# One hand-written order for the front, the first v unit and the convolution stage of a hybrid mixer layer

## The chip, the cores and the metric

The kernel runs on one core of a Trainium2 chip. The metric is the device time of one execution in microseconds; the time of the kernel before is the median of three runs. A profile of one execution gives the instructions of each engine: PE (TensorE products), PEld (its weight loads), DVE (VectorE), ACT (ScalarE), POOL (GpSimd) and SP (SyncE, which here only issues DMAs).

## The reference, cut to what matters

One layer works on 1024 latent tokens and 256 context tokens of width 1024:

```
shift, scale, gate = split(silu(c) @ w_ada + b_ada, 3)          # context: the same with c_ctx
h  = rms_norm(x)   * (1 + scale)   + shift
hc = rms_norm(ctx) * (1 + scale_c) + shift_c
qkv_a, z_a, a_raw, b_raw, q_b, k_b, v_b, z_b, gates = split(h @ w_in)
# branch A: conv of 5 taps + silu on qkv_a, l2 norm of q and k, gated delta rule in chunks, both directions,
#           with decay from a_raw and beta from b_raw
# branch B: rms norm and rotary position of q_b, k_b, two softmax maps p0 - lam * p1 against v_b
out = x + gate * ((sigmoid(g_a) * (y_a @ w_oa) + sigmoid(g_b) * (y_b @ w_ob)) @ w_out)
```

`lam` comes from four vectors lambda_q1, lambda_k1, lambda_q2, lambda_k2, and the rotary tables from `rope` and the norm weights of q and k. All is float32; a product is made of three products of high and low halves (`hi*hi`, `hi*lo`, `lo*hi`).

## The kernel before, in words

The program is straight line code, and every engine executes its instructions in order. The order comes from one of two sources. Most of the program is ordered by a planner of the framework, which plays through an own model of the times. Sections inside `tc.manual_schedule` keep the order in which the Python code issues; there the code has *streams* (generators that yield an engine, a price in us, what the step waits for, and the instruction), and `turn_flow` takes the stream whose next step can start first by those prices, with a bias of each stream between steps of the same engine. `DV2` and `POOL` in a price mean that the two exclude each other.

The stages around the change:

- **Front** (`front`, L229). SP loads `c`, `c_ctx`, the modulation weights `w_ada` in four units (0 to 3) of two halves of 1 MB, x in tiles of 128 tokens (groups of 4, 4 and 2 tiles, the last the context), the first v weights `w`, and the small rows `rw` (b_ada, norm weights, conv_w). The letters of `"01osw23xy"` are the order of the loads. `rms(g)` squares x on ACT (L303), takes the inverse root on DVE (L180 to L185, twelve instructions with L304) and scales x (L307). `modulation(u)` multiplies c by `w_ada` on PE (L320; L318 for units 2 and 3), copies the row (L321), transposes it in another bank (L328 or L330) and adds the bias (L333, L335). `turn(g, k)` transposes one eighth of the width of a token group (L344) and modulates it: high half on ACT (L346), full value on DVE (L347), low half on DVE or POOL in turn (L348).
- **First v unit** (`tok_unit`, L422, with `before`): ten tiles of 128 tokens times 288 columns (256 of v, 32 of the decay and beta inputs), 24 products a tile. The first four tiles are taken in three parts of the width. The planner orders the front and this unit. `v_out` (L638 to L643) casts the high half on ACT, subtracts the low half on DVE and stores both.
- **Convolution stage** (`conv_start`): hand order. 24 tiles of q, k and v of branch A: products on PE, four of five taps on DVE, silu, norms, stores. Side streams are the weights, `gates()` (decay and beta, in a bank of `self.pt`) and `gate_row()`. `lam_setup` (L1406 to L1417) stands just ahead of it, in the planner's part.
- **Second v unit**: planner's order again. `gdn_first` issues the first loads and ACT's decay instructions (L1050, exponential L1052) of the scan, `qk_tables` builds the rotary tables (loads L616 and L619, small products L622, eight products L627, store L630), and `v_unit(1)` makes five banks of two tiles each, copied out through one pair of buffers `ch0`, `cl0` with the same `v_out`.
- **Scan section**: hand order again, with pieces of k, v and q of branch B between (`part_flow`), and the Gram products of the delta rule (`gram`, in `gdn_prep`).

The banks of PSUM that the front, gates and norms use were one pool of three buffers under one tag, given out in turn:

```
self.pt = self.spool(cp, "ptr", 3, space=PSUM)
...
for u in range(4):
    modulation(u)
    turn(0, 2 * u)
    turn(0, 2 * u + 1)
```

Of the kernel before, what the change touches and what calls it, by code (L numbers as in the profile page):

```python
# [8 lines left out]
F32 = mybir.dt.float32  # L9
# [8 lines left out]
P = 128  # L18
# [25 lines left out]
class Block:  # L44
# [143 lines left out]
    def setup(self):  # L188
# [30 lines left out]
        self.tbd = self.dp.tile([P, 1024], F32, name="tbd")  # L219
# [7 lines left out]
    def front(self, st, early):  # L227

        nc, a, cp = self.nc, self.a, self.cp  # L229
        fs, ft = self.spool(st, "fs", 1, side="right"), self.spool(st, "ft", 2, side="right")  # L230
        fx = [self.spool(early, "fx0", 4)] + [self.spool(st, f"fx{i}", n, side="right") for i, n in ((1, 4), (2, 2))]
        fq = self.pt
        groups = (range(0, 4), range(4, 8), range(8, NT))
        xt, wa = {}, {}
# [4 lines left out]
        def load_x(t):  # L239
            nc.sync.dma_start(xt[t], a["x"][0, t * P:(t + 1) * P, :] if t < NL else  # L240
                              a["ctx"][0, (t - NL) * P:(t - NL + 1) * P, :])

        def load_ada(u):

            for i in range(2):
                if u == 0:
                    wa[u, i] = self.wab[0].tile([P, KT, W], F32, tag=("wh", "wl")[i], name="wa")
                elif u == 1:
                    wa[u, i] = self.hc.tile([P, KT, W], F32, tag=f"s2{i}", name="wa")
                else:  # L250
                    if i == 0:
                        wa[u, 2] = self.hp.tile([P, KT, 512], F32, tag=f"s1{u - 2}", name="wa")
                    wa[u, i] = wa[u, 2][:, :, i * W:(i + 1) * W]
                nc.sync.dma_start(wa[u, i], a["w_ada"][0, :, i * D + u * W:i * D + (u + 1) * W].rearrange(
                    "(k p) n -> p k n", p=P))

        rows = fs.tile([16, P], F32, name="rows")
        nc.sync.dma_start(rows[0:8, :], a["c"].rearrange("o (k p) -> (o k) p", p=P))
        nc.sync.dma_start(rows[8:16, :], a["c_ctx"].rearrange("(k p) -> k p", p=P))
        for o in "01osw23xy":  # L260
            if o == "s":
                rw2 = fs.tile([26, P], F32, name="rw2")
                nc.sync.dma_start(rw2[0:24, :], a["b_ada"].rearrange("o (k p) -> (o k) p", p=P))
                nc.sync.dma_start(rw2[24:25, :], a["gdn_norm_w"])
                nc.sync.dma_start(rw2[25:26, :], a["diff_norm_w"])
                rw3 = fs.tile([120, P], F32, name="rw3")
                nc.sync.dma_start(rw3, a["conv_w"].rearrange("o j (k p) -> (o j k) p", p=P))
            elif o in "0123":
                load_ada(int(o))
            elif o == "w":  # L270
                self.ahead = self.load_w(self.wcols(C_VB), True)
            else:
                for t in groups["oxy".index(o)]:
                    load_x(t)
        sil = fs.tile([16, P], F32, name="sil")
        nc.scalar.activation(sil, rows, AF.Silu)
        tp = fq.tile([P, 512], F32, tag="tr", name="tp")
        nc.tensor.transpose(tp[:, 0:16], sil, self.ident[:16, :16])
        cT = self.cT = cp.tile([P, 16], F32, name="cT")
        nc.vector.tensor_copy(cT, tp[:, 0:16])  # L280
        smallT = cp.tile([P, 184], F32, name="smallT")

        def smalls():
            tp = fq.tile([P, 512], F32, tag="tr", name="tp")
            nc.tensor.transpose(tp[:, 16:42], rw2, self.ident[:26, :26])
            nc.tensor.transpose(tp[:, 64:184], rw3, self.ident[:120, :120])
            nc.vector.tensor_copy(smallT[:, 16:42], tp[:, 16:42])
            nc.vector.tensor_copy(smallT[:, 64:184], tp[:, 64:184])

        self.gdn_g, self.diff_g = smallT[:, 40:41], smallT[:, 41:42]  # L290
        self.convw = lambda j, t: smallT[:, 64 + j * 24 + t:64 + j * 24 + t + 1]
        c2 = cT.rearrange("p (s k) -> p s k", s=2)
        pad = fs.tile([P, KT, 32], F32, name="pad")
        nc.gpsimd.memset(pad, 0.0)
        nc.vector.tensor_copy(pad[:, :, 0:2].rearrange("p k s -> p s k"), c2)
# [3 lines left out]
        def rms(g):  # L299
            cnt = len(groups[g])  # L300
            ss = fs.tile([P, 4], F32, tag="ss", name="ss", bufs=2)
            for j, t in enumerate(groups[g]):
                nc.scalar.activation(junk, xt[t], AF.Square, accum_out=ss[:, j:j + 1])  # L303
            nc.vector.tensor_scalar(ss[:, :cnt], ss[:, :cnt], 1.0 / D, EPS, ALU.mult, ALU.add)  # L304
            rs = self.rsqrt(fs, ss[:, :cnt], "xr")
            for j, t in enumerate(groups[g]):
                nc.vector.tensor_scalar_mul(xt[t], xt[t], rs[:, j:j + 1])  # L307

        def modulation(u):
            mp = fq.tile([P, 512], F32, tag="tr", name="mp")  # L310
            split = u >= 2
            n = P if split else 2
            mrow = fs.tile([P, 2, W], F32, tag="mrow", name="mrow")
            for i in range(2):
                for k in range(KT):
                    if split:
                        j = k % 4
                        nc.tensor.matmul(mp[32 * j:32 * j + 32, i * W:(i + 1) * W], pad[:, k], wa[u, i][:, k], start=k < 4, stop=k >= 4)  # L318
                    else:
                        nc.tensor.matmul(mp[:2, i * W:(i + 1) * W], c2[:, :, k], wa[u, i][:, k], start=k == 0, stop=k == KT - 1)  # L320
                nc.vector.tensor_copy(mrow[:n, i], mp[:n, i * W:(i + 1) * W])  # L321
            if u == 0:
                smalls()
            mt = fq.tile([P, 512], F32, tag="tr", name="mt")
            for i in range(4):
                half = mrow[:n, i // 2, i % 2 * P:i % 2 * P + P]
                if split:
                    nc.tensor.matmul(mt[:, i * 2:i * 2 + 2], half, self.fold[:, 0:2], start=True, stop=True)  # L328
                else:
                    nc.tensor.transpose(mt[:, i * 2:i * 2 + 2], half, self.ident[:2, :2])  # L330
            m = mods[:, :, 2 * u:2 * u + 2]
            bias = smallT[:, 16:32].rearrange("p (i k) -> p i k", i=2)[:, :, 2 * u:2 * u + 2]
            nc.vector.tensor_tensor(m, mt[:, 0:8].rearrange("p (i k s) -> p i k s", i=2, k=2),  # L333
                                    bias.unsqueeze(3).to_broadcast([P, 2, 2, 2]), ALU.add)
            nc.vector.tensor_scalar_add(m[:, 1], m[:, 1], 1.0)  # L335

        def turn(g, k):
            grp, nn = groups[g], len(groups[g]) * P
            th, tl, o = self.hsel(grp[0])
            s = 1 if grp[0] >= NL else 0  # L340
            sh, sc = mods[:, 0, k, s:s + 1], mods[:, 1, k, s:s + 1]
            pt = fq.tile([P, 512], F32, tag="tr", name="pt")
            for j, t in enumerate(grp):
                nc.tensor.transpose(pt[:, j * P:(j + 1) * P], xt[t][:, k * P:(k + 1) * P], self.ident)  # L344
            hf = ft.tile([P, 512], F32, tag="hf", name="hf")
            nc.scalar.activation(th[:, k, o:o + nn], pt[:, :nn], AF.Identity, bias=sh, scale=sc)  # L346
            nc.vector.tensor_scalar(hf[:, :nn], pt[:, :nn], sc, sh, ALU.mult, ALU.add)  # L347
            (nc.vector, nc.gpsimd)[k % 2].tensor_tensor(tl[:, k, o:o + nn], hf[:, :nn], th[:, k, o:o + nn].bitcast(F32),  # L348
                                                        ALU.subtract)

        rms(0)
        for u in range(4):
            modulation(u)
            turn(0, 2 * u)
            turn(0, 2 * u + 1)
        def before(t0):
            g = 1 + t0 // 4
            if t0 in (0, 4):
                self.hgroup(g)
                rms(g)  # L360
            if g < 3:
                for k in range(t0 % 4 * 2, t0 % 4 * 2 + 2):
                    turn(g, k)
        return before
# [1559 lines left out]
```

## Time and profile before

| | |
|---|---|
| median of three runs | 2060.99 us (2059.3 to 2066.39) |
| profiled execution | 2064.51 us, span 2062.7 us |
| busy share of the span | PE 96%, PEld 84%, DVE 69%, ACT 51%, POOL 33% |
| DMA | 336.45 MB, 163 GB/s over the span |
| mean granted TensorE clock | 0.982 |

A row of a timeline is start, duration, engine, line, operation, output and inputs, and in brackets how long the engine had been idle before it and what released it. A row of a grouped view is the group, its count, busy time and mean duration (ns), then the idle time before its members. The view by stretch has busy time and count for each engine, then the granted clock, the share of the DMA engines and GB/s. Products are pipelined, so the rows of PE overlap.

### The profile page before, as it was taken

Reading aid. Unit: us, or ns where it says so; the run is one execution under the profiler, and the core shown is the slowest. Engines: PE = TensorE matmul, PEld = TensorE weight load, DVE = VectorE, ACT = ScalarE, POOL = GpSimd, SP = SyncE. Lnnn points to the kernel's source line nnn. Section 1 sums busy time; section 2 is a strip of 40 time slices with the busy share of each in tenths; the row PEclk is TensorE's granted clock in tenths of the full one; section 3 lists DMA queues with packets and bytes.
Section 4 is the critical chain, followed back from the end, with each engine's and each line's share of the span. In section 5 each row is a group of like instructions: output and inputs, shape, how many; then the busy total and the mean of one; then the engine's idle time right before and its main releaser. Section 6 shows DMA issues by size and latency. Waiting matters only on the chain.

```text
span 2062.7 us, 38349 instructions
## 1 busy us (share of the span) xinstructions
PE 1970.5 (96%) x14231; PEld 1729.1 (84%) x14231; DVE 1418.1 (69%) x3611; ACT 1053.9 (51%) x2176; POOL 686.6 (33%) x601
## 2 busy tenths in 40 slices
PE   6999999979999998999899999999899999989999
PEld 3888888879999997878778888887788888877899
DVE  3798989747876895557556786237789899864532
ACT  3443435343325543566456754448678888763210
POOL 1200000014531331323233333235566767654122
PEclk9999999989999999999999999999999999999999
DMA  9226452665446546755764764857575766326442
GB/s 313 86 84 159 123 115 75 133 178 159 140 138 210 174 157 175 238 168 199 196 218 139 245 190 131 248 146 220 140 195 133 202 172 159 103 83 203 144 154 82
DMA packets 391742, 336.45 MB, mean 163 GB/s; under 512 B 144399, under 2 KB 343665, under 8 KB 391555
## 3 DMA queue, kind: packets, MB, share of 16 engines
q1 hardware_dynamic: 328675, 274.22, 46.0%
q10 hardware_dynamic: 62880, 59.78, 9.5%
q8 instruction: 112, 1.84, 0.4%
q14 instruction: 75, 0.61, 0.1%
HBM read 222.14 MB, written 111.79 MB: 162 GB/s over the span
## 4 chain that ended last, share of the span: by engine, by line
PE 70%; DMA 10%; DVE 9%; ACT 5%; issue 3%; POOL 1%; SPq 1%; ACTq 0%; DVEq 0%; POOLq 0%
PE mm L55 37%; PE chain L55 5%; PE mo L55 4%; PE s L55 4%; PE v L55 4%; DVE S L1505 3%; PE out L55 3%; PE mm L422 3%; PE ma L55 3%; DMA hx<-in_w_in_dram 2%; ACT S L1518 2%; PE t L58 2%; DMA ma<-ma 1%; PE gram L55 1%; DMA x<-xd 1%
## 5 line engine op out<-in xcount | busy, mean ns | idle before, releaser
L55 PE MATMUL mm<-hs,wh 128*128 128x512 f32 (+1 forms) x2048 | 646.0, 390 | 0.0
L55 PEld LDWEIGHTS mm<-hs,wh 128*128 128x128 f32 x2048 | 374.1, 191 | 57.6 <-issue 0.9
L55 PE MATMUL mm<-hs,wl 128*128 128x512 f32 (+1 forms) x1024 | 401.0, 392 | 0.0
L55 PE MATMUL mm<-wh,hs 128*128 128x256 f32 x1472 | 274.1, 286 | 0.0
L1505 DVE TENSOR_SCALAR_CACHE_REDUCE S<-s,rsq 128x512 f32<-128x512 f32 (+1 forms) x384 | 241.6, 654 | 32.3 <-PE s L55 28.9
L55 PEld LDWEIGHTS mm<-wh,hs 128*128 128x128 f32 x1472 | 231.4, 192 | 0.4
L55 PEld LDWEIGHTS mm<-hs,wl 128*128 128x128 f32 x1024 | 195.0, 190 | 29.2 <-issue 0.9
L1542 POOL TENSOR_TENSOR S<-S 128x1280 f32<-128x1280 f32 x64 | 188.8, 2952 | 91.4 <-ACT S L1535 88.9
L55 PE MATMUL mm<-wl,hs 128*128 128x256 f32 x736 | 210.4, 286 | 0.0
L1518 ACT ACTIVATE S<-S,mn 128x1280 f32<-128x1280 f32 x128 | 174.7, 1366 | 34.4 <-DVE mn L1517 33.9
L55 PE MATMUL s<-kk,qh 128*128 128x512 f32 (+1 forms) x384 | 144.9, 378 | 3.6 <-DVE S L1505 3.3
L523 DVE SCALAR_TENSOR_TENSOR ac<-xc,smallT,ac 128x1284 f32<-128x1284 f32 (+1 forms) x96 | 138.9, 1448 | 11.3 <-ACT ac L521 10.5
L55 PEld LDWEIGHTS mm<-wl,hs 128*128 128x128 f32 x736 | 141.2, 192 | 0.3
L55 PE MATMUL s<-kk,ql 128*128 128x512 f32 (+1 forms) x384 | 133.6, 358 | 0.0
L1579 DVE TENSOR_TENSOR al<-t,ah 128x512 fp32r<-128x512 f32 (+1 forms) x192 | 107.6, 592 | 10.6 <-ACT ah L1574 10.0
L511 ACT COPY xc<-mm 128x512 f32<-128x512 f32 (+1 forms) x64 | 34.0, 534 | 145.9 <-PE mm L55 134.8
L1574 ACT CAST ah<-t 128x512 fp32r<-128x512 f32 (+1 forms) x192 | 89.9, 515 | 30.6 <-PE t L58 29.3
L1101 DVE TENSOR_TENSOR tmp<-ab,ts 80x31 f32<-80x31 f32 (+15 forms) x248 | 98.8, 398 | 8.4 <-DMA ab<-da 2.8
L508 POOL MEMSET xc<- 128x2 f32 (+1 forms) x64 | 3.6, 100 | 290.9 <-ACT sq L562 150.7
L58 PE MATMUL t<-ct,S 128*128 128x128 f32 x640 | 95.7, 275 | 3.2 <-POOL S L1542 1.6
L1279 DVE SCALAR_TENSOR_TENSOR S<-S,egl,chain 128x128 f32<-128x128 f32 x128 | 43.1, 344 | 76.4 <-PE chain L55 73.5
L1266 ACT ACTIVATE vd<-chain,edk 128x128 f32<-128x128 f32 x144 | 52.1, 368 | 84.6 <-PE chain L55 79.2
(280 smaller groups left out, 4804.9 us busy)
## 6 DMA issues: line engine op xcount, KB each, us to landing
wr<-in_w_in_dram ACTq DMA_DIRECT2D x42, 512.0 KB
hx<-in_w_in_dram ACTq DMA_DIRECT2D x64, 256.0 KB
X<-gcd SPq DMA_DIRECT2D x16, 640.0 KB
kd<-col SPq DMA_DIRECT2D x40, 256.0 KB
xd<-X SPq DMA_DIRECT2D x16, 640.0 KB
x<-xd SPq DMA_DIRECT2D x80, 128.0 KB
kk<-kd SPq DMA_DIRECT2D x32, 320.0 KB
wa<-in_w_ada_dram SPq DMA_DIRECT2D x8, 1024.0 KB
```

Source lines behind the costliest of these rows:

```text
L55: self.nc.tensor.matmul(out, lhsT, rhs, start=start, stop=stop)
L58: self.nc.tensor.transpose(out, src, self.ident[:src.shape[0], :src.shape[0]])
L422: nc.tensor.matmul(pt[:, j * W:j * W + n], ht[:, k, ts], wt[:, k, :n], start=k == i == 0, stop=k == KT - 1 and i == 2)
L523: t = yield DV2, 1.21e-3 * wd, [t], lambda: nc.vector.scalar_tensor_tensor(ac[:, :wd], xc[:, j:j + wd], self.convw(j, x["ct"]), ac[:, :wd] ...
L1101: t = yield DV2, n * w / 960.0 + 0.08, [t, t1], lambda: V.tensor_tensor(tv, ab[:, j + 1:, j:j + 1].to_broadcast([80, n, w]), ts[:, j, :w]. ...
L1266: td = yield ACT, 0.251, [t], lambda: nc.scalar.activation(vd, pc[:, 1], AF.Copy, scale=self.edk[:, c, g:g + 1])
L1279: t = yield DVE, 0.263, [t], lambda: V.scalar_tensor_tensor(Sn, S, self.egl[:, c, g:g + 1], pc[:, 2], ALU.mult, ALU.add)
L1505: e = yield DVE, 0.675 if m == 512 else 0.408, [e, self.sfree[c].get(n - 4 + c)], lambda: self.nc.vector.tensor_scalar(x["S"][c][:, o:o + ...
L1518: x["x"].append((yield ACT, 1.36, [e], lambda: nc.scalar.activation(S, S, AF.Exp, bias=x["mn"][:, c:c + 1], scale=-1.0, accum_out=w["l0"][ ...
L1542: e = yield POOL, 2.9, [e], lambda: self.nc.gpsimd.tensor_tensor(S0, S0, S1, ALU.add)
L1574: e = yield ACT, 0.48 if nb == 4 else 0.27, [t, y["old", k]], lambda: self.nc.scalar.copy(y["ah", k][:, :, q], pv)
L1579: t = yield DVE, 0.603 if k < 2 else 0.322, [e, y["old", k]], lambda: self.nc.vector.tensor_tensor(y["al", k][:, :, q], pv, y["ah", k][:, ...
```

## The change

The front, the first v unit and the convolution stage lie in one `manual_schedule`. Every step of the front is a stream with prices; the rotary tables and lambda become streams of the convolution stage beside the gates. In detail:

- Loads: the letters are `"0s1xw23yk"`: the small rows come after unit 0's weights, and the load of the first convolution weights (`k`, once the v weights are split) is one of them. The split of those has both low halves on DVE (before: one on POOL, one on DVE).
- Modulation: products, copy, the two transposes and the bias add of a half share one bank, half after half.
- The three banks get names (`tr0` to `tr2`) and a list `pfree` with the time from which each is free; a stream that needs one waits for the list.
- `turned` (high, full and low half) is queued by even and odd k; low halves of even k are DVE's, of odd k POOL's (as before).
- Tables: both are stored to DRAM (`tbd` has two parts); the one for k is loaded again after the convolution stage. They use the buffer `graw` of the gate row, which therefore starts after them. The gate temporaries `gtmp` and `gr` share a buffer.

```
-                        self.lam_setup()
...
+                    with tc.manual_schedule(engines={E.PE, E.DVE, E.Activation, E.Pool, E.SP}):
+                        with ExitStack() as st, ExitStack() as sw:
+                            self.wv = self.spool(sw, "wv")
+                            with ExitStack() as early:
+                                self.front(st, early, self.wcols(kv[0][1]))
+                        with ExitStack() as st:
...
                             self.conv_start(kv, C_VB + W)
                 first, head = self.gdn_first(gr, zr)
-                self.qk_tables()
+                tb = self.tk.tile([P, 2, 2, NL, 32], F32, tag="tb", name="tb")
+                nc.sync.dma_start(tb.rearrange("p a b t f -> p (a b t f)"), self.tbd[1])
+                self.rope["k"] = tb, None
```

The front's streams, and those of the convolution stage (the number is the bias):

```
+        for g, b in ((loads(), 0), (modulation(), 1), (smalls(), 1), (rms(), 2), (weights(), 1.5), (turns(), 1), (self.forever(turnq[0]), 1.2),
+                     (self.forever(turnq[1]), 1.2), (self.forever(evq), 3), (main(), 9)):
+            self.stream(g, b)
+        self.turn_flow(lambda: "end" in T and not evq and 0 in self.parts_)
...
-        self.stream(self.gates(), 0.5)
+        for g, b in ((self.gates(), 0.5), (self.lam_setup(), 0.6), (self.qk_tables(), 4)):
+            self.stream(g, b)
```

One half of the modulation, and the products of the v unit:

```
+                for i in range(2):
+                    yield lambda: ("wa", u, i) in T
+                    o = i * W
+                    for k in range(KT):
...
+                    t = yield DVE, 0.42, [t], lambda: V.tensor_copy(mrow[:n, i], mp[:n, o:o + W])
+                    for q in range(2):
+                        t1 = yield PE, 0.17 if u >= 2 else 0.09, [t], lambda: self.mm(
+                            mp[:, o + 2 * q:o + 2 * q + 2], mrow[:n, i, q * P:q * P + P], self.fold[:, 0:2]) if u >= 2 else self.tr(
+                            mp[:, o + 2 * q:o + 2 * q + 2], mrow[:n, i, q * P:q * P + P])
...
+        def main():
...
+                        for k in ks:
+                            yield lambda: ("h", g, k) in T and ("w", k // 4) in T
...
+                                e = yield PE, 0.133, [T["h", g, k], T["w", k // 4], b], lambda: self.mm(
+                                    pt[:, :W + 32], ht[:, k, o:o + P], wt[:, k], k == i == 0, k == KT - 1 and i == 2)
+                        if KT - 1 in ks:
+                            evq.append(evac(t, pt, e))
```

The tables as a stream:

```
+            tc.append((yield DMA, 0.4, [], lambda: nc.sync.dma_start(cs[:, i], a["rope"][i].rearrange("(t p) f -> p t f", p=P))))
+        for n, (nm, mul) in enumerate((("q", -(64.0 ** -0.5)), ("k", 1.0))):
+            g0 = tk.tile([P, 64], F32, tag="g0" + nm, name="g0")
+            t = yield DMA, 0.2, [], lambda: nc.sync.dma_start(g0, a[f"{nm}_norm_w"].to_broadcast([P, 64]))
+            t = self.later(t, 4.0)
...
+                    te = yield DV2, 0.4, [tg, tc, to], lambda: V.tensor_tensor(
+                        tb[:, i, hf], cs[:, i], g[:, hf].unsqueeze(1).to_broadcast([P, NL, 32]), ALU.mult)
+            to = yield DMA, 1.5, [te], lambda: nc.sync.dma_start(self.tbd[n], tb.rearrange("p a b t f -> p (a b t f)"))
+            to = self.later(to, 4.0)
+        self.rope, self.tb_t = dict(g=g), to
```

More of the change, by code (lines that the diff above doesn't have):

```diff
@@ L257, in front @@
[L257 to L280, printed above, removed]
-        smallT = cp.tile([P, 184], F32, name="smallT")
[L283 to L288, printed above, removed]
+        rows, rw2, rw3 = (fs.tile([n, P], F32, name=i) for i, n in (("rows", 16), ("rw2", 26), ("rw3", 120)))
@@ L309, in modulation @@
[L309 to L314, printed above, removed]
-                for k in range(KT):
[L316 to L364, printed above, removed]
+        self.pfree, self.slot_t = [(i, None) for i in range(3)], [None, None]
+        turnq, evq, wv = ([], []), [], [self.wv.tile([P, KT, W + 32], F32R, tag=t, name=t) for t in ("wh", "wl")]
@@ new lines, in evac @@
+        def evac(t, pt, e):
+            vt, old = [self.tv.tile([P, 2, W], F32R, tag=i, name="vt") for i in ("vh", "vl")], self.slot_t[t % 2]
+            e1 = yield ACT, 0.31, [e, old], lambda: nc.scalar.copy(vt[0][:, 0], pt[:, :W])
+            e2 = yield DVE, 0.38, [e1, old], lambda: V.tensor_tensor(vt[1][:, 0], pt[:, :W], vt[0][:, 0].bitcast(F32), ALU.subtract)
+            e3 = yield DVE, 0.15, [e], lambda: V.tensor_copy(self.abt[:, t], pt[:, W:W + 32])
+            free.append([e1, e2, e3])
+            self.slot_t[t % 2] = ends = []
+            for i, x in enumerate((e1, e2)):
+                ends.append((yield DMA, 0.5, [x], lambda: nc.sync.dma_start(
+                    self.vd[i, t * P:(t + 1) * P, 0:W], vt[i][:, 0].bitcast(F32))))
@@ L390, in load_w, with unit @@
         return hi, lo
[L392 to L406 removed]
+    def unit(self, src, work, then):
+        cur, self.ahead = self.ahead, self.load_w(then)
+        work(*cur)
@@ L441, in work @@
                 emit(t0, pt)
[L442 to L444 removed]
+        return self.wcols(c0), work
     CB = 5
```

391 lines of the change are left out of this document (241 added, 150 removed).

## The prediction

> **What bounds the kernel now.** I read the page first, then busy time by stretch with the cuts where the chain of waits changes its character, then the chain itself, and last the timeline of each engine in the two places that stood out.
>
> ```profile
> span 2062.7 us, 38349 instructions
> ...
> PE 1970.5 (96%) x14231; PEld 1729.1 (84%) x14231; DVE 1418.1 (69%) x3611; ACT 1053.9 (51%) x2176; POOL 686.6 (33%) x601
> ```
>
> The PE (TensorE matmul row) is busy for 96% of the span, so a change that leaves the products alone can only remove idle PE time, and idle time there moves all that follows. By stretch (us; busy time and count of PE, PEld, DVE, ACT, POOL; granted clock; DMA share; GB/s):
>
> ```profile
> 0.00:94.74 94.74, 72.90 (x483) 55.19 (x484) 52.18 (x125) 36.88 (x60) 22.35 (x20) 0.91 0.62 205
> 94.74:409.33 314.59, 314.59 (x1583) 266.00 (x1583) 274.88 (x388) 134.55 (x162) 3.61 (x64) 1.00 0.46 116
> 409.33:445.21 35.88, 35.88 (x300) 35.67 (x298) 14.61 (x16) 15.95 (x30) 5.43 (x3) 1.00 0.74 189
> 445.21:458.94 13.73, 0.00 (x1) 0.03 (x1) 8.74 (x20) 7.80 (x18) 3.65 (x2) 0.63 0.38 134
> ```
>
> The convolution stage (94.74 to 409.33) has no idle PE at all, DVE has 314.59 - 274.88 = 39.7 us to spare in it. The front with the first v unit (0 to 94.74) leaves PE idle for 21.8 us, and what is busy there runs partly at a lower clock. Between the second v unit and the scan section PE stands still for 13.73 us. These two places are what the change can touch.
>
> **The front: why it takes 92.7 us.** The nine convolution products already inside the stretch are taken off: 94.74 - 9 x 0.2265 (the order's own price of one) = 92.7 is where the v unit would have ended alone.
>
> ```profile
> L55 PE MATMUL mm<-hs,wh 128*128 128x512 f32 x6 | 2.0, 393 | 0.0
> L55 PE MATMUL mm<-hs,wl 128*128 128x512 f32 x3 | 1.2, 394 | 0.0
> ```
>
> Timeline of the front (start, duration, idle before it and its cause):
>
> ```profile
> 7.45 5.76 PE L320 MATMUL mp<-wa,cT 128*2 128x256 f32 x16 [2.18 <-DMA wa<-in_w_ada_dram]
> 13.71 3.62 PE L320 MATMUL mp<-wa,cT 128*2 128x256 f32 x16 [0.51 <-DVE mrow L321]
> 21.98 0.21 PE L285 MATMUL tp<-ct,rw 26*128 26x26 f32 x1 [4.65 <-DMA rw<-in_diff_norm_w_dram]
> 24.99 2.61 POOL L389 TENSOR_TENSOR wl<-wr,wh 128x1152 fp32r<-128x1152 f32 x1 [23.93 <-ACT wh L388]
> 25.03 2.59 DVE L185 SCALAR_TENSOR_TENSOR xry<-xrt,xry 128x4 f32<-128x4 f32 x1
> 29.58 1.41 DVE L307 TENSOR_SCALAR x<-x,xry 128x1024 f32<-128x1024 f32 x2
> 36.12 1.53 DVE L347 TENSOR_SCALAR hf<-pt,mods 128x512 f32<-128x512 f32 x2 [1.10 <-ACT hs L346]
> 37.57 0.68 DVE L348 TENSOR_TENSOR hs<-hf,hs 128x512 fp32r<-128x512 f32 x1
> 38.86 0.40 PE L422 MATMUL mm<-wh,hs 128*128 128x288 f32 x1
> 69.58 0.65 ACT L638 CAST vt<-mm 128x256 fp32r<-128x256 f32 x2 [0.98 <-PE mm L422]
> ```
>
> PE executes in order, and the order puts the small rows' transpose (L285) behind the first modulation unit: it waits 4.65 us, until 21.98, for rows that were issued behind 6 MB of weights and x. The second modulation unit (two halves of 3.62 us) comes after that and after the wait for the scaled x (ready at 30.99), so the first v product is at 38.86. The first token group is not complete until just before 69.58, when the first v tile is copied out. From there PE is continuous; the chain has it on PE from 71.32 on, 92.7 - 71.3 = 21.4 us.
>
> ```profile
> 71.32 0.67 PE mm L422 x3
> ...
> 94.74 27.35 PE mm L55 x143
> ...
> 438.13 7.08 PE mm L55 x59
> 445.21 13.73 issue
> 458.94 2.05 PE gram L55 x8
> ```
>
> **Edit 1, the front under the hand order.** Removed: the order in which PE waits for rows, for x and for DVE in turn. The small rows are issued behind 2 MB rather than 6 MB, so unit 0 ends soon after its weights. Its products run as now until 17.3. Each half now shares one bank with its two transposes, so product, copy, transposes and add alternate; the row at 13.71 shows one such hand-over at 0.51 us, four of them and the copy I take at 1.5 us a half. Unit 1 then ends at about 18.8 + 2 x (3.62 + 1.5) = 29, or 32 if its copies queue behind the DVE instruction that stalls until 27.6: either way no later than the scaled x, which stays at 31 (its chain, squares then DVE, is not changed, and the POOL split of the v weights at 24.99 still meets it). Transposes, ACT, DVE and the low half follow: first v product near 35 instead of 38.9.
>
> ```profile
> L307 DVE TENSOR_SCALAR x<-x,xry 128x1024 f32<-128x1024 f32 x10 | 6.9, 749 | 0.1
> L184 DVE SCALAR_TENSOR_TENSOR xrt<-xrt,ss 128x4 f32<-128x4 f32 x6 | 1.0, 163 | 0.2
> L321 DVE COPY mrow<-mp 128x256 f32<-128x256 f32 x4 | 1.7, 420 | 0.8 <-PE mp L318 0.8
> L639 DVE TENSOR_TENSOR vt<-mm,vt 128x256 fp32r<-128x256 f32 x8 | 3.3, 415 | 0.3 <-DMA vd<-vt 0.2
> L389 DVE TENSOR_TENSOR wl<-wr,wh 128x1024 fp32r<-128x1024 f32 x1 | 1.2, 1217 | 0.0
> L348 POOL TENSOR_TENSOR hs<-hf,hs 128x512 fp32r<-128x512 f32 x8 | 13.9, 1733 | 34.3 <-DVE hf L347 29.6 <-DVE xry L181 4.7
> ```
>
> From here DVE decides. One pair of k (rows 36.12 and 37.57) costs it 1.53 + 0.68 = 2.2 us; the first group's four pairs 8.8, units 2 and 3 about 2.4 (four copies of 0.42 and the small adds), the v weights' low half 1.4: 12.6 us, so the group is complete at 31 + 1.5 + 12.6 = 45, say 47 with some waits, instead of 69. What is then left for DVE: scaling six tiles 6 x 0.75 = 4.5, two chains of 12 small instructions at 0.16 plus gaps 4.8, the second group's pairs 8.8, the context group's about 6 (half as wide, but not half the time: I take 1.5 a pair), ten evacuations of 0.42 and 0.18 6.0, both low halves of the first convolution weights 2.4 (one of them is POOL's today): 32.5 us. About 4 of it fits in before 47. Stalls against POOL, of which the row at 25.03 is one, I put at about 4 again. DVE is through at 47 + 32.5 = 79; the last two tiles' evacuations and part of the weight split lie behind the last product, so PE ends at about 77. PE alone would take 21.4 us from 47, so 69 to 71 is the floor. Gain: 92.7 - 77 = 15.7, between 92.7 - 71 = 22 and, if the group is only complete at 54, 92.7 - 84 = 8.
>
> [...]
>
> **Edit 2, lambda, gates and rope tables as side streams of the convolution.** Moved into it: eight table products and four small ones, and their loads.
>
> ```profile
> L627 DVE TENSOR_TENSOR tb<-ropecs,g x8: 413/418/2633, 441.8 to 449.2; 128x256 f32<-128x256 f32 x8
> ...
> 430.12 4.20 SPq L616 DMA_DIRECT2D ropecs<-in_rope_dram  x2
> 434.37 3.56 SPq L619 DMA_DIRECT2D g<-in_q_norm_w_dram  x1
> 438.04 0.37 SPq L643 DMA_DIRECT2D vd<-vt  x1
> ...
> 432.77 5.97 ACT L1050 ACTIVATE X<-X,gcc 128x128 f32<-128x128 f32 x20 [10.81 <-DMA X<-gcd]
> 442.17 1.27 ACT L1052 ACTIVATE X<-X 128x1280 f32<-128x1280 f32 x1
> ...
> 441.54 0.27 DVE L622 TENSOR_SCALAR g<-g 128x32 f32<-128x32 f32 x2 [18.40 <-DMA g<-in_q_norm_w_dram]
> 458.14 0.69 DVE L639 TENSOR_TENSOR vt<-mm,vt 128x512 fp32r<-128x512 f32 x1 [2.29 <-DMA vd<-vt]
> 460.28 0.58 ACT L638 CAST vt<-mm 128x512 fp32r<-128x512 f32 x1 [2.27 <-DMA vd<-vt]
> ```
>
> In the convolution they cost DVE 8 x 0.418 + 4 x 0.135 = 3.9 us against 39.7 spare, PE nothing; if that cover were gone, 3.9. The gate row waits for the tables (one buffer), and nobody needs it before the last phase. Gates and lambda ran there or just ahead already: nothing.
>
> Where they are taken away: DVE stood for 18.40 us at L622, in front of the second v unit's first low half; SP spent 4.20 + 3.56 us on the tables' loads ahead of the first v store. Evacuations use one pair of buffers, so each waits for the store before it: from DVE's half (458.14) to the next ACT half (460.28) 2.1, plus ACT's 0.58: about 2.8 us a turn. The Gram product at 458.94 starts when the low half at 458.14 has ended: it waits for a bank of the v unit. Without the tables the first low half can follow its cast at once, and the first store leaves at 438.0 - 7.8 = 430.3 (a load of the finished table, 0.5 MB, takes their place on SP; one issue like that at 438.04 is 0.4 us). What is late next is ACT: if the 20 decay instructions and both exponentials keep their place ahead of the second cast, that comes at 443.4, and the fourth low half ends 2 x 2.8 + 0.6 + 0.7 later, near 450.5: 5.3 us of idle stay, 8.4 go. If the casts come first, all 13.7 go. I take 9 (nearer the first, as nothing moves ACT's loads).
>
> ```profile
> 460.00:470.00 10.00, 10.00 (x78) 10.00 (x78) 5.24 (x14) 4.47 (x14) 1.26 (x1) 0.88 0.42 142
> 470.00:480.00 10.00, 10.00 (x87) 9.98 (x86) 8.18 (x24) 3.54 (x8) 4.32 (x4) 1.00 0.28 91
> ```
>
> After the idle time the clock is granted at 0.88 and 78 instead of 87 products are done: 9 x 0.115 = 1 us, which goes too where the idle time does. [...]
>
> **Sum.** 15.7 + 9 + 1 = 25.7 us. The profiled execution took 2064.51 us, 1.8 around its span, and lies 3.5 above the median of 2060.99; the stretches are the same in all, so the median becomes 2060.99 - 25.7 = 2035.
>
> **Rivals.** (a) Only the front is gained: ACT's order or the v stores keep the Gram product at 459. For it: the 10.7 us of ACT work ahead of the second cast; against it: the 18.40 us of DVE are gone in any order. 2060.99 - 16 = 2045. Chance 0.13. [...] Chance 0.13. (c) Slower: DVE's wait moves along. If in the convolution the lambda, norm and table instructions stand in DVE's order ahead of loads that SP has not issued yet, DVE stops there as it did at L622, the buffers of four tiles fill, and PE stops too. One stop of 18.4 us is covered by the 39.7 spare; it decides, against the 25.7 gained, from 39.7 + 25.7 = 65 us of stops, and four loads (lambda, rope, two norms) at 18.4 each make 74: 2035 + 74 - 40 = 2069. For it: DVE is in order and the loads' times in the order are prices, not measurements; against it: the gates' loads stand in the same queue today and PE has no idle time there. Chance 0.06. (d) The two orders come out alike: 2060. Chance 0.04. The forecast: 0.64.
>
> Range: 22 + 14.7 = 37 gives 2024 at the low end; the high end takes in (a) and (b), 2051. Within 0.3% (6 us, about what a measurement tells here) is (d); slower is (c) and part of what I cannot name, 0.07; faster 0.89.
>
> **What would show it.** Right: the first convolution product near 77, PE without idle time from there to the scan section, the L622 pair in the convolution, no stretch of over 6 us without PE near 430, the Gram product within 6 us of the end of the first 48 products. Wrong: the first group's last low half after 55; PE idle in the convolution; DVE idle over 10 us there before a table product; the Gram product still behind a v low half by more than 8 us; or a gap that reappears further on, at the waits of the first scan steps.

## The result, and the profile after

The changed kernel takes 2054.59 us (median of its runs, 2049.53 to 2060.42) against 2061.38 us of the kernel before in the same runs: ratio 0.9965, interval 0.9952 to 0.9978, some 7 us faster. The forecast was 2035 with a range of 2024 to 2051.

The page after, its first lines, and the stretches, cut at the first convolution product, the end of the convolution, the end of the first products of the second v unit and the first Gram product:

```profile
span 2049.1 us, 38360 instructions
...
PE 1968.3 (96%) x14231; PEld 1726.7 (84%) x14231; DVE 1419.5 (69%) x3616; ACT 1053.8 (51%) x2176; POOL 682.3 (33%) x600
```

```profile
0.00:92.89 92.89, 74.31 (x476) 55.43 (x476) 53.83 (x131) 35.50 (x59) 17.95 (x19) 0.93 0.60 200
92.89:411.04 318.15, 316.39 (x1592) 267.39 (x1591) 277.08 (x399) 135.52 (x162) 3.55 (x64) 1.00 0.48 121
411.04:446.91 35.87, 35.87 (x299) 35.67 (x298) 12.42 (x13) 17.67 (x35) 5.46 (x3) 1.00 0.73 207
446.91:454.90 7.99, 0.01 (x2) 0.04 (x1) 5.47 (x11) 5.94 (x14) 3.66 (x2) 0.72 0.33 110
460.00:470.00 10.00, 10.00 (x84) 10.00 (x84) 7.18 (x21) 5.80 (x15) 2.79 (x2) 0.97 0.31 105
```

The front still ends at 92.9 us (before 92.7). In the convolution PE now stands idle for 1.76 us (318.15 - 316.39); before, it had no idle time there. The idle time ahead of the Gram product went from 13.73 to 7.99 us, and 84 products instead of 78 are done in the 10 us from 460. The profile after is a short execution (2050.87 us), the one before a long one (2064.51); single executions differ by several us in the later stages (below), so I read the traces up to the Gram product and the medians for the rest.

**The front.** Timeline of DVE, ACT and PE in it:

```profile
30.25 0.75 DVE L391 TENSOR_SCALAR x<-x,xry 128x1024 f32<-128x1024 f32 x1
35.61 0.81 DVE L412 TENSOR_SCALAR hf<-pt,mods 128x512 f32<-128x512 f32 x1 [1.26 <-ACT hs L409]
40.91 0.38 PE L55 MATMUL mm<-wh,hs 128*128 128x288 f32 x1
49.26 0.68 DVE L415 TENSOR_TENSOR hs<-hf,hs 128x512 fp32r<-128x512 f32 x1
49.85 1.27 DVE L383 TENSOR_SCALAR ss<-ss 128x4 f32<-128x4 f32 x1
52.83 1.23 DVE L313 TENSOR_TENSOR wl<-wr,wh 128x1024 fp32r<-128x1024 f32 x1
54.05 1.22 DVE L313 TENSOR_TENSOR wl<-wr,wh 128x1024 fp32r<-128x1024 f32 x1
55.15 0.37 ACT L442 CAST vt<-mm 128x256 fp32r<-128x256 f32 x1 [4.09 <-PE mm L55]
55.90 2.73 DVE L391 TENSOR_SCALAR x<-x,xry 128x1024 f32<-128x1024 f32 x4
69.48 0.85 PE L55 MATMUL mm<-wh,hs 128*128 128x288 f32 x2 [2.31 <-DVE hs L415]
81.71 0.41 DVE L415 TENSOR_TENSOR hs<-hf,hs 128x256 fp32r<-128x256 f32 x1
```

```profile
57.00:69.50 12.50, 6.63 (x45) 4.79 (x44) 11.49 (x25) 7.33 (x13) 4.80 (x4) 0.94 0.21 72
69.50:74.40 4.90, 4.56 (x16) 4.02 (x17) 4.72 (x11) 0.00 (x0) 1.06 (x1) 0.50 0.00 0
74.40:92.89 18.49, 18.46 (x138) 17.91 (x136) 8.26 (x23) 5.94 (x13) 3.39 (x4) 0.99 0.22 72
```

The first group is early, nearly as forecast: first full value at 35.6, first v tile copied out at 55.15 instead of 69.58. The first v product is not early: 40.91 (38.86 before), as PE's order has transposes and products of units 2 and 3 ahead of it. From 57 us on PE runs dry. The second group's x is scaled at 55.90 to 58.6, where before it was done by 55.2: its squares lie between the first group's turns, its root chain begins with a stall beside POOL (1.27 us for four elements) and lets two weight splits of 1.2 us through. The expectations below call such stalls the lock with POOL. Four of DVE's small instructions, whose likes take 0.16 us, ended within 0.02 us of one of POOL's here: 25.16 for 2.58 (POOL's split, 25.10 for 2.62), 49.85 for 1.27 (its low half, 49.42 for 1.68), 64.10 for 1.27 (64.08 for 1.28) and 66.52 for 1.05 (66.28 for 1.28); before, the rows at 24.99 and 25.03 ended so, at 27.60 and 27.62. Its turns last until 73, and the products go tile by tile, so PE gets three products for each turn: 6.63 us of work in 12.50 us, then 4.90 us at a granted clock of 0.50. The 18.49 us of products behind that are the rest, and they end at 92.9.

How much of PE's own work was left can be counted. The first row is of the kernel before, from the moment at which the forecast took its 21.4 us of remaining PE work; the second is of the change, from 47 us, where the forecast put them:

```profile
71.32:94.74 23.42, 23.42 (x175) 23.12 (x176) 14.61 (x36) 9.20 (x19) 7.26 (x7) 1.00 0.27 89
47.00:92.89 45.89, 39.65 (x272) 36.72 (x271) 33.34 (x78) 19.14 (x35) 12.24 (x10) 0.93 0.17 58
```

Before, 175 less nine of the convolution are 166 PE instructions; now 272 are left, because the first group's products run only behind its early low halves, until 57 us.

The rows of before to which this compares (timeline of the kernel before, the second group's x, and for the next part the gate row):

```profile
52.47 2.74 DVE L307 TENSOR_SCALAR x<-x,xry 128x1024 f32<-128x1024 f32 x4
...
240.35 1.02 PE L55 MATMUL mg<-gacc,ct 128*1 128x512 f32 x2
```

**The convolution.** The table steps, and the gate row that now comes behind them:

```profile
107.55 0.18 DVE L685 TENSOR_SCALAR g<-g 128x32 f32<-128x32 f32 x1
145.36 0.42 DVE L690 TENSOR_TENSOR tb<-ropecs,g 128x256 f32<-128x256 f32 x1
280.22 1.18 DVE L882 TENSOR_TENSOR wl<-wr,wh 128x1024 fp32r<-128x1024 f32 x1
281.43 0.68 DVE L667 TENSOR_TENSOR grow<-mg,grow 1x512 f32<-1x512 f32 x1
282.16 1.02 PE L55 MATMUL mg<-gacc,ct 128*1 128x512 f32 x2 [1.76 <-DVE grow L667]
```

The tables themselves cost PE nothing that these rows show. The gate row does: its second pair of products needs the bank that DVE's add (L667) empties, that add stands behind a weight split, and PE waits 1.76 us in order. Before, it ran at 240.35 with no idle time in front.

**The gap.** The chain, then ACT and DVE:

```profile
446.91 7.99 issue
454.90 2.05 PE gram L55 x8
```

```profile
434.33 5.96 ACT L1113 ACTIVATE X<-X,gcc 128x128 f32<-128x128 f32 x20 [10.66 <-DMA X<-gcd]
444.89 0.56 ACT L700 CAST vt<-mm 128x512 fp32r<-128x512 f32 x1
445.49 0.69 DVE L701 TENSOR_TENSOR vt<-mm,vt 128x512 fp32r<-128x512 f32 x1 [19.90 <-ACT vt L700]
450.52 0.57 ACT L700 CAST vt<-mm 128x512 fp32r<-128x512 f32 x1
453.39 0.58 ACT L700 CAST vt<-mm 128x512 fp32r<-128x512 f32 x1 [1.13 <-DMA vd<-vt]
454.10 0.69 DVE L701 TENSOR_TENSOR vt<-mm,vt 128x512 fp32r<-128x512 f32 x1 [2.29 <-DMA vd<-vt]
```

DVE no longer waits for a load, but for ACT: the second cast comes at 444.89, behind the 20 decay instructions and the exponentials, and the last turns wait for stores.

### The profile page after: what moved, and what is told of

Read it like the earlier page. It is cut to its first block, busy times and chain, and to the rows that moved or that the text cites. A ratio compares the mean times of both kernels' runs of the same rounds, so it can differ in the third digit from the quotient of the medians.

```text
span 2049.1 us, 38360 instructions
## 1 busy us (share of the span) xinstructions
PE 1968.3 (96%) x14231; PEld 1726.7 (84%) x14231; DVE 1419.5 (69%) x3616; ACT 1053.8 (51%) x2176; POOL 682.3 (33%) x600
## 4 chain that ended last, share of the span: by engine, by line
PE 72%; DVE 10%; DMA 8%; ACT 5%; issue 2%; POOL 1%; SPq 1%; ACTq 0%; DVEq 0%; POOLq 0%
PE mm L55 40%; PE chain L55 5%; PE mo L55 4%; PE s L55 4%; PE v L55 4%; DVE S L1569 3%; PE out L55 3%; PE ma L55 3%; ACT S L1582 2%; PE t L58 2%; DMA ma<-ma 1%; PE mm L501 1%; PE gram L55 1%; DVE al L1643 1%; DMA x<-xd 1%
## 5 line engine op out<-in xcount | busy, mean ns | idle before, releaser
L55 PE MATMUL mm<-wh,hs 128*128 128x256 f32 (+1 forms) x1632 | 313.2, 290 | 2.6 <-DVE hs L415 2.6
L55 PEld LDWEIGHTS mm<-wh,hs 128*128 128x128 f32 x1632 | 260.8, 194 | 3.8 <-DVE hs L415 3.4
L55 PE MATMUL mm<-wl,hs 128*128 128x256 f32 (+1 forms) x816 | 236.1, 289 | 0.0
L55 PEld LDWEIGHTS mm<-wl,hs 128*128 128x128 f32 x816 | 158.3, 194 | 0.3
```

What stands on the lines that cost most here:

```text
L55: self.nc.tensor.matmul(out, lhsT, rhs, start=start, stop=stop)
```

## The experiments

All kernels are compared with the kernel before in the same runs. First convolution product, idle PE ahead of the first Gram product and its start are from the profiles, in us.

| kernel | first conv. product | idle | Gram | median (before) | ratio, interval |
|---|---|---|---|---|---|
| the change | 92.89 | 7.99 | 454.90 | 2054.59 (2061.38) | 0.9965, 0.9952 to 0.9978 |
| 1 front only | 92.70 | 12.27 | 457.23 | 2062.44 (2063.96) | 0.9991, 0.9977 to 1.0005 |
| 2 tables only | 92.28 | 7.99 | 453.53 | 2057.48 (2063.96) | 0.9965, 0.9951 to 0.9979 |
| 3 four parts | 91.40 | 8.52 | 452.13 | 2057.44 (2063.96) | 0.9955, 0.9936 to 0.9973 |
| 4 late split | 91.81 | 8.27 | 454.10 | 2060.63 (2063.96) | 0.9981, 0.9962 to 1.0001 |
| 5 no chain | 88.15 | 7.99 | 451.76 | 2056.89 (2066.13) | 0.9960, 0.9946 to 0.9975 |
| 6 x early | 96.06 | 7.99 | 458.07 | 2062.12 (2066.13) | 0.9991, 0.9975 to 1.0008 |
| 7 as 3, one execution | 88.87 | 8.01 | 449.08 | 2050.77 (2066.13) | none |
| 8 two pairs | 93.47 | 0.27 | 447.77 | 2048.45 (2066.13) | 0.9921, 0.9901 to 0.9941 |
| 9 gate first | 93.47 | 8.43 | 454.17 | 2060.30 (2065.02) | 0.9974, 0.9958 to 0.9989 |
| 10 gate, pairs | 92.82 | 0.84 | 445.92 | 2052.68 (2065.02) | 0.9937, 0.9919 to 0.9955 |
| 11 gate, pairs, parts | 90.10 | 1.26 | 443.42 | 2046.25 (2065.02) | 0.9913, 0.9894 to 0.9933 |
| 12 tables, pairs | 92.43 | 0.21 | 445.90 | 2049.38 (2065.02) | 0.9932, 0.9908 to 0.9955 |
| 13 no chain, all | 89.75 | 0.40 | 442.32 | 2043.08 (2066.93) | 0.9895, 0.9868 to 0.9922 |
| 14 chain first | 91.95 | 0.41 | 444.44 | 2047.94 (2066.93) | 0.9906, 0.9879 to 0.9934 |

In kernels 2 and 12, as in the kernel before (91.90), some v products still follow the first convolution product, so their first column is about 0.8 us early against the others: 92.7 is the figure for the kernel before with that taken off.

**1 and 2, the two edits apart.** Kernel 1 is the change with `qk_tables` at its old place (lambda stays a stream); kernel 2 is the kernel before with lambda and tables as streams.

```
1  -            self.stream(... (self.qk_tables(), 4)) in the convolution
   +                self.qk_tables()                    behind gdn_first
2  +        for g, b in ((self.gates(), 0.5), (self.lam_setup(), 0.6), (self.qk_tables(), 4)):
   +            self.stream(g, b)
```

> The change without its rope tables: front, first v unit, lambda and gates under the hand order, the rope tables built where they were. My theory (in the front DVE and PE were only rearranged; PE is starved of the second token group and pays later what it gained early): first convolution product at 92.9 us as in the whole change, DVE's 18 us stand at the norm weights back at about 441, Gram product at 459, time within 2 us of the kernel before. Rival (the front did gain, and the tables in the convolution took it back): first convolution product still at 92.9 in the trace, but the convolution ends 1.5 us or more earlier than in the whole change, and the time is 3 us or more under the kernel before.

> The kernel before with only the second edit: rope tables and lambda as side streams of the convolution stage, the front in the planner's order. Theory: the Gram product comes 4 to 6 us earlier (idle PE ahead of it 8 us instead of 13.7), and the time is 4 to 7 us under the kernel before, that is the whole of what the change brings. Rival (the two edits need each other): no more than 2 us.

The front alone is within the interval of no change; the tables alone have the whole gain. So Edit 2 works, and Edit 1 is worth nothing that can be measured here.

**3, the second group's tiles in four parts of the width**, as the first group has them (run 7 is a further execution of the same kernel):

```
-for ts, parts in (...,) + tuple(((t,), (range(KT),)) for t in range(4, NT)):
+for ts, parts in (..., (range(4, 8), ((0, 1), (2, 3), (4, 5), (6, 7))), ((8,), (range(KT),)), ((9,), (range(KT),))):
```

> The change with the second token group's four tiles taken in four parts of the width, as the first group's are in three, so that PE has products of four tiles for each eighth that DVE finishes. Theory (PE in order stands at tile 4 for the last eighth while the products of tiles 5 to 7 could run): 3 tiles x 21 products x 0.133 = 8.4 us come forward, the first convolution product is at 84 to 86 instead of 92.9, and the time falls by up to 8 us against the whole change (2046 to 2050) unless it is given back at a later wait. Rival (DVE and its lock with POOL set the end of the front): first convolution product within 2 us of 92.9.

> A second look at the kernel of the third experiment (the second group's four tiles in four parts of the width), for its trace alone: the first convolution product again within 0.5 us of 91.4, the granted clock between 60 and 72 us again at 0.5 to 0.7 if the half clock belongs to this order of work, near 1.0 if it was this one execution.

The stretches from 60 and from 70 us, first of run 3, then of run 7:

```profile
60.00:70.00 10.00, 7.68 (x35) 6.05 (x34) 8.88 (x18) 5.86 (x10) 4.30 (x4) 0.59 0.19 65
70.00:80.00 10.00, 10.00 (x70) 9.72 (x70) 6.67 (x15) 2.05 (x5) 1.82 (x2) 0.90 0.01 3
```

```profile
60.00:70.00 10.00, 6.29 (x46) 5.10 (x44) 9.21 (x18) 5.80 (x10) 4.86 (x4) 1.00 0.20 67
70.00:80.00 10.00, 9.98 (x74) 9.16 (x74) 8.58 (x19) 3.65 (x7) 2.70 (x3) 1.00 0.00 1
```

One program, two executions: in run 3 PE looks busier and did 35 products at a clock of 0.59, in run 7 46 at 1.00. The first convolution product came at 91.40 and at 88.87, not at 84 to 86: the parts are worth 1.5 to 4.0 us, and the two executions, which differ in the clock, lie 2.5 us apart. The executions end 13 us apart (spans 2062.2 and 2049.0), 3.0 us of it by the Gram product (452.13, 449.08): one profile can't weigh a few us of the later stages. Neither shows the wait at the gate row (PE is busy for all of 280 to 290 us in run 3 and of 270 to 300 in run 7) although the row still follows the tables, so the wait seems to hang on where the row falls among DVE's steps.

**4, the first convolution weights' split held back until the context's turns:** `yield lambda: ("kr", 1) in T and ("h", 2, 3) in T`.

> The change with the split of the first convolution weights held back until half of the context group is turned, so that its two low halves (2.4 us of DVE) no longer stand inside the second group's inverse root. Theory: x of the second group is scaled 2.4 us earlier (56.2 instead of 58.6) and the first convolution product comes 2 to 3 us earlier. Rival (something else, the last square on ACT or POOL's lock, holds the scaling): no change in the first convolution product.

The second group's x is scaled from 52.74 instead of 55.90, but the front ends only 1.1 us earlier, below what was expected; no gain in time.

**5, the second group's x without its own root chain.** It is scaled with the first group's inverse roots; its own squares and chain run behind, for nobody. Its result leaves out the second group's own roots, so the kernel serves to measure only.

```
+                if g == 1:
+                    for j, t in enumerate(groups[g]):
+                        T["xs", t] = yield DVE, 0.69, [T["x", t], e0], lambda: V.tensor_scalar_mul(xt[t], xt[t], y0[:, j:j + 1])
```

> The change, with one dependency taken out: the second token group's x is scaled with the first group's inverse roots as soon as it has landed, and its own squares and root chain still run, behind it, for nobody (so the second group's result is not the reference's). All engines do the same work. Theory 1, the front's end hangs on the second group's scaled x (ready at 58.6 us in the profile of the change, 55.2 before): x scaled by 48 to 51, the second group's turns run in 51 to 65 instead of 59 to 73, first convolution product at 84 to 86 instead of 92.9, time 6 to 8 us below the change (2047 by a before of 2061). Rival 2, DVE's total of work sets it: the work is the same, first convolution product at 91.5 to 93, time as the change. Rival 3, PE's order and half clock set it: as in the four-part kernel, 1 to 2 us earlier.

With the same work for every engine the front ends 4.7 us earlier, at 88.15: the late x is one limit, and not DVE's sum of work alone; 84 to 86 was too much. The time is that of the change. Part of it was lost again in the convolution, at the gate row (PE's timeline, then the 4 us behind the wait):

```profile
277.43 1.02 PE L55 MATMUL mg<-gacc,ct 128*1 128x512 f32 x2 [1.77 <-DVE grow L674]
```

```profile
278.00:282.00 4.00, 4.00 (x13) 3.05 (x12) 3.96 (x5) 1.05 (x1) 0.00 (x0) 0.58 1.20 303
```

Here the same wait is followed by a clock of 0.58. From the first convolution product to the end of the stage this execution takes 319.6 us, the profile of the change 318.0, and those of kernels 9 and 10, without the wait, 316.2: 3.4 us are lost here, 1.8 in the change.

**6, the second group's x loaded ahead of units 2 and 3:** the letters `"0s1xwy23zk"`.

> The change with one other order of loads: the second group's four tiles of x (2 MB) ahead of modulation units 2 and 3 (4 MB), the context's x behind them. Theory 1 (the second group's scaled x): it is scaled by about 47, units 2 and 3 land some 5.7 us later (2 MB at 365 GB/s), so the first group is complete at 56 to 57 instead of 51, but the second group's turns follow without a wait, in 57 to 69 instead of 59 to 73: first convolution product 2 to 4 us earlier, 89 to 91. Rival (the front hangs on the last modulation unit and on DVE's sum of work): first convolution product 2 to 5 us later, 95 to 98, time 2 to 5 us above the change.

The rival holds: units 2 and 3 come later, and the first scaled tile at 45.4 is followed by the last only at 55.1, between the first group's late turns. First convolution product 3.2 us later, and the time is no better, 0.9991. With this order of the loads the front gains nothing.

**8, two pairs of buffers in the second v unit:**

```
-        vt = [self.tk.tile([P, 2, W], F32R, tag=t, name="vt") for t in ("ch0", "cl0")]
+        vt = [... for t in (("ch0", "cl0"), ("ch1", "cl1"))[t0 // 2 % 2]]
```

> The change with two pairs of buffers, in turn, for the second v unit's evacuation (before: one pair, so that each cast waits for the store of the one before). Theory: the wait for the stores goes, and the order puts the second cast ahead of the 20 decay instructions: PE's idle time ahead of the first Gram product falls from 7.99 to under 1.5 us, Gram product at 447 to 448.5 instead of 454.9. If what is gained there is kept to the end, the time is 6 to 7.5 us below the change (ratio to before near 0.993); rival: given back in the scan section's first steps or near 610 us, ratio as the change, 0.9955 to 0.997. Second rival: the Gram product waits for the decay matrices instead, 450 to 452.

```profile
445.83 1.05 ACT L700 CAST vt<-mm 128x512 fp32r<-128x512 f32 x2
446.43 1.29 DVE L701 TENSOR_TENSOR vt<-mm,vt 128x512 fp32r<-128x512 f32 x2 [19.66 <-ACT vt L700]
447.77 1.16 PE L55 MATMUL gram<-kq 128*128 128x128 f32 x8 [0.27 <-DVE vt L701]
```

Two casts now stand ahead of the decay instructions, the next two follow each other, and the Gram product starts 0.27 us behind DVE. It is the best single edit, 0.9921, and most kernels below have it.

**9 to 12, the gate row first, the sum, and the old front.** In 9 `gate_row` no longer waits for `tb_t`, and `qk_tables` does; 10 is 8 and 9, 11 is 10 and the four parts; 12 is kernel 2 with two pairs of buffers.

> The change with the gate row ahead of the rope tables (the tables wait for the shared buffer, not the gate row). Theory: the wait of the gate row's second product for DVE's add stays in PE's order but falls where it fell before the change (before 245 us), behind DVE instructions that are through in time; the convolution stage has no idle PE at 270 to 290 (1.76 us in the profile of the change, and 1.77 us with a granted clock of 0.58 behind it in the profile without the chain), its end comes 1.8 us earlier relative to its start; time 2 us below the change, up to 5 where the half clock is saved as well. Rival: the wait moves along with the gate row, PE stands as long at its new place: no difference.

> The change with the gate row first and two pairs of buffers in the second v unit, together. If the two are separate places that add up: 2 us below the kernel with two pairs alone, ratio to before 0.990 to 0.992, Gram product within 1.5 us of the second v unit's last product. Rival: one of them is given back in the other's place or later: 0.992 to 0.994.

> The kernel before this one in the list, and the second token group's four tiles in four parts of the width (first convolution product 88.9 and 91.4 in the two profiles of that edit alone, 92.9 in the change). If the 1.5 to 4 us of the front are kept once the gate row no longer stops PE in the convolution: 1.5 to 4 us below it, ratio to before 0.988 to 0.991. Rival: the front's gain is lost again in the convolution or later: no difference.

> The kernel before, with only the tables and lambda as side streams and two pairs of buffers in the second v unit; its front is the old one, ordered by the planner. If the new front is worth nothing, this is as fast as the change with two pairs: ratio to before 0.991 to 0.994. If the new front is worth its 10 us of earlier products after all, somewhere off the places looked at: 0.995 or more.

In 9 and 10 PE has no idle time in the convolution (from 270 to 290 us it is busy for all of it), so the wait is gone. In time this can't be seen: 0.9974 and 0.9965, 0.9937 and 0.9921 overlap. Kernel 11 is below 10 in the same runs, 2046.25 against 2052.68, more than the 2.7 us of its front; the intervals overlap. Kernel 12 bears out experiment 1: with the old front the time is that of kernels 8 and 10, within the intervals.

**13 and 14, both limits of the front at once.** 13 is 11 with 5's edit (so it too leaves out the second group's own roots), and the weights' split behind the second group's turns; 14 is 11 with that split and the root chains ahead of the turns (bias 0.8 instead of 2).

> Both limits of the front taken out at once, with the gate row first and two pairs of buffers: the second group's x scaled with the first group's inverse roots as soon as it has landed (its own squares and roots run behind for nobody, so the second group's result is not the reference's), its four tiles in four parts of the width, and the split of the first convolution weights behind its turns. If the late scaled x and the tile-by-tile order are what held the front (4.7 us for the one alone, 1.5 and 4.0 for the other): first convolution product at 83 to 86 instead of 92.9, and, as the gate row no longer stops PE, 4 to 7 us below the kernel with gate row, pairs and parts. If a third thing holds the front (DVE's sum of work with POOL's lock, the half clock): 87 to 89.

> The kernel with gate row first, two pairs and four parts, and in the front the root chains ahead of the turns where both could go (bias 0.8 instead of 2) and the split of the first convolution weights behind the second group's turns. It leaves nothing out. If the second group's scaled x holds the front: x scaled by 55 to 56 instead of 58.6, first convolution product at 86.5 to 88.5 (90.1 without these two), 1.5 to 3 us below that kernel. Rival: the turns of the first group are pushed back as much as the chain comes forward: 89 to 91, no difference in time.

Not 83 to 86 but 89.75 in kernel 13, so more is left than those two. DVE and PE of 13, then the stretch behind, and all from 47 us on:

```profile
65.92 2.35 DVE L313 TENSOR_TENSOR wl<-wr,wh 128x1024 fp32r<-128x1024 f32 x2
68.67 0.18 DVE L452 COPY abt<-mm 128x32 f32<-128x32 f32 x1
68.99 0.58 PE L55 MATMUL mm<-wh,hs 128*128 128x288 f32 x1 [2.22 <-DVE xrt L392]
```

```profile
69.00:72.00 3.00, 3.00 (x12) 3.00 (x13) 2.58 (x17) 0.00 (x0) 0.00 (x0) 0.50 0.42 132
47.00:89.75 42.75, 38.60 (x274) 36.43 (x274) 31.45 (x75) 22.17 (x40) 12.71 (x10) 0.96 0.16 51
```

The unit has five banks (`CB`). A tile of the second group waits for the evacuation of one of the first, and those copies stand on DVE behind the two weight splits; PE waits 2.22 us and then runs at a granted clock of 0.50 for 3 us, 12 products where 22 fit at the pace of the change from 74.40 on (138 in 18.46 us). But the last row says more: of the 42.75 us PE is busy for 38.60, so what mostly sets the end in 13 is PE's own products. In 14 the x is scaled at 53.1 to 55.9 as expected, but the rival holds: the end, 91.95, is no better than in 11 (clock 0.69 and 0.80 in the two stretches from 60), nor is the time. Not settled is how much of what lies between PE's own work (until about 82 us, worked out below) and these ends an order that computes everything could have; kernels 11 and 14 have the lowest medians of those, and their intervals lie below those of both kernels of the case.

## Why the prediction was wrong, by its own steps

- **Early front (right, but for the first v product).** Unit 1 by 29 to 32, first group complete near 47 to 54: the products of units 0 and 1 run to 28, the group's last low halves end at 50 to 51. The first v product was put near 35; it came at 40.91, later than before.
- **DVE through at 79 (near: 82.1).** Its last low half is at 81.71, and the stalls beside POOL cost no more than the 4 us allowed: three small instructions took 1.27, 1.27 and 1.05 us instead of 0.16. That all of POOL's 13.9 us come to stand on DVE, which is behind the 2051 of (b) in the range, no run shows; the runs showed those three, and turns on DVE that took as long beside POOL's low halves as without (0.81 us at 69.54, POOL's 68.91 for 1.66; 0.80 at 68.03, POOL idle). DVE was not as late as before, though of the two places only the tables' was gained.
- **"PE ends at about 77", with "PE alone would take 21.4 us from 47" as its floor (the step that failed, 15.7 us, measured 0).** The 21.4 us were read off the chain from 71.32 on, and two things were true there that are not true at 47. First, PE had worked off nearly all products of the first group while it waited for the group's last parts: 166 PE instructions were left, against 272 at 47 in the new order. At the pace of before (21.4 us for 166) these take about 35 us, an estimate, so PE alone ends near 82, not at 69 to 71, and at most 10.7 us could be gained. Second, the second group's x had been scaled since 55.2 and its turns ran just ahead of the products. After the change the first v tile comes some 14 us earlier, but the second group's x 3.4 us later, and nothing stood between: PE did 6.63 us of work in 12.50, and 4.90 us at half clock (0.50). From 47 on that makes 6.2 us of idle PE (45.89 - 39.65) and some 4.6 us more (39.65 - 35, so an estimate too) for the same products at a lower clock (0.93 in that row), which leads from 82 to 92.9. I had named as next late the evacuations behind the last product; next late were PE's own products of the first group, then the second group's chain of squares, roots and turns, with the tile-by-tile products behind it (experiments 3 and 5), and behind that the banks (13).
- **Tables in the convolution cost 0 (right for the tables, wrong for what they move).** "The gate row waits for the tables, and nobody needs it before the last phase" looked at who waits for the row, not at what the row's own wait stops: PE's order, 1.76 us, and 3.4 us with the clock of 0.58 behind it in run 5. Kernel 9 takes the wait away, but its time doesn't show the gain.
- **The gap (mechanism right, size off).** Named was ACT as next late, with 5.3 us to stay by it; I then took 9 us as the gain, nearer to the whole. Measured: 5.7 gone, 7.99 left, as the second cast came at 444.89 instead of 443.4, the third cast only 5.6 us later, behind the key pieces and more decay instructions on ACT, and not one turn of 2.8. The clock behind it: 6 products of 0.115, 0.7 us for 1 forecast.
- **The sum.** 25.7 forecast; 0 + 5.7 + 0.7 less the gate row's 1.8 is 4.6, against 6.8 by the medians (4.5 to 9.9 by the interval); kernel 2, without the new front and the gate row's wait, has 5.4 us at the Gram product, against 6.5. By the edits apart some 6 us are from the tables' place (kernel 2) and 0 from the front (kernel 1).

## What to carry to other kernels

When a stage is made early, write down for the next stage when each of its inputs is ready today and whether the old wait was hiding that work; a remainder read off a chain (so many us of PE from here) holds only with the inputs that were ready there, and with the work that the engine had already done under the old wait: count the instructions that are left. An unneeded result still costs what its own wait stops in an engine's order: 1.76 us of PE for the gate row. One buffer pair whose store is waited for can be worth more than reordering what stands before it: 0.9921 against 0.9965 for one line of code.

## What the runs showed of the hardware

Half clock followed pauses of about 2 us in three profiles: 0.50 over the 4.90 us from the end of a 2.31 us wait on (the change), 0.50 over the 3 us behind a 2.22 us wait (run 13), 0.58 over the 4 us behind 1.77 us (run 5). It did not follow 1.76 us in the convolution of the change (1.00 over the 4 us from 282 on), and the same 10 us of one program had 0.59 or 1.00 (runs 3 and 7). These rows give neither a length of pause that decides nor the length of the slow stretch behind it.
